# Linear attention by levels of four parts, with TensorE's order around it fixed by dependences

## The chip, the cores and the metric

One Trainium2 chip, one core of it. The program is launched once and computes both layers of the trunk. The metric is the device time of that launch in microseconds (us), lower is better. The core has TensorE (PE, with its weight loads as PEld), VectorE (DVE), ScalarE (ACT), GpSimd (POOL) and the sync engine SP, which issues most DMAs. Each works through its own instructions strictly in program order, and waits on semaphores for the others.

## The reference, cut to what matters

Each of two layers is a SwiGLU half-step, a token mixing and another SwiGLU half-step, on 512 tokens of 1024 channels. Only the mixing is touched:

```python
h = rmsnorm(x, mix_norm[l])
q_a, k_a, v_a, q_b, k_b, v_b, r_b, g_lr, gate_a, gate_b = split_cols(h @ w_in[l], IN_SPLITS)
o_a = swa_attention(...)       # 8 heads of 64, softmax with sinks over a window of 128 tokens
log_a = log_sigmoid(g_lr @ gla_w_gate[l] + gla_gate_bias[l]) / 16
o_b = gla_attention(q_b, k_b, v_b, log_a)   # 4 heads, keys of 128, values of 256
o_b = rmsnorm(o_b) * silu(r_b)
merged = sigmoid(gate_a) * (o_a @ w_proj_a[l]) + sigmoid(gate_b) * (o_b @ w_proj_b[l])
x = x + merged @ w_out[l]

# inside gla_attention, with b the running sum of log_a: for t >= s
attn[t, s] = sum_c q[t, c] * k[s, c] * exp(b[t, c] - b[s, c])
o = attn @ v + (q * exp(b)) @ S     # S: the state that is carried over chunks
```

The decay exp(b[t] - b[s]) differs by channel c, so attn is no single matrix product. The kernel splits it by levels: for a pair t, s on two sides of a boundary r, exp(b[t] - b[r]) goes to q and exp(b[r] - b[s]) to k, and the product of the two is one matmul for all pairs that a boundary of this level parts.

## The kernel before

All tensors lie transposed, channels on the 128 partitions and the 512 tokens along the free axis, in four blocks of 128 tokens. Weights are float32, split into a high and a low part in a narrower format, so that each dense product is three matmuls (`mul3`, L182; operands float32r). The split is one ScalarE copy (`whi`, L114) and one VectorE subtraction (`wlo`, L115) for each 512 columns, in class `Weights`, which also issues the DMA of 1 MB on SP (L133). The small matmuls of the attention and of the linear attention are float32; the hardware runs such a matmul in two passes, which appear as two records, so that "x8" in a row is four matmuls.

A tile scheduler orders the instructions of each engine ahead of time: the earlier something is written, the higher its rank; what stands later in the code is taken where the earlier has not got its operands. `with tc.high_priority` lifts weight loads ahead. PSUM has eight buffers, four of tag `mm` (the dense products, `acc()`) and four of tag `sm` (all the small ones, `psum()`); a matmul into an `sm` buffer waits until the engine that reads its former contents is through.

The mixing, `mix` (L420), is written in this order:

- q and k of the softmax attention, their rotation by `cos` and `sin` (columns of the constants `cst`), `values(0)`.
- The attention, L571 to L613: eight steps (four blocks, two groups of four heads). A step is a chain: eight score matmuls (L581, operands float32r, so one record each), four VectorE reductions with mask and maximum (L586), two tiny ones (L589, L590), five ScalarE exponentials (L591, L594), VectorE sum, reciprocal and four scalings (L595 to L599), TensorE transposes (L606), two VectorE copies (L608), the product with v (L612) and its split (L613).
- The decays b of the linear attention (L616 to L631), q and k of its four heads (`pair`, L635: 48 dense matmuls each), `values(1)` and `values(2)` (L508: 96 dense matmuls of 384 columns each).
- The linear attention, head by head, L647 to L737: seven levels of two parts (widths 64 to 1). A level is VectorE subtractions (L655, L659), an exponential (L198), GpSimd's product with k (L662, into one of three buffers `ke`), VectorE's with q (L666), four matmuls of 64 columns (L675; L671 for width 64) and a masked copy into `attn` (L678). After the levels the diagonal (L683), states (L691 to L712), output (L721, L723), its copy by VectorE (L725), squares, norm and a scaling by VectorE (L736).
- `gate` and the products of the softmax attention's output with its projection, four times (L748 to L759), then everything else (L762 on).

Since gates and projections stand later, the scheduler puts them between the steps of the linear attention, as it puts the q and k products and the values between the steps of the softmax attention.

Of the kernel before, what the change touches and what calls it, by code (L numbers as in the profile page):

```python
# [10 lines left out]
F32R = mybir.dt.float32r  # L11
# [6 lines left out]
P = 128  # L18
# [12 lines left out]
LEVELS = (64, 32, 16, 8, 4, 2, 1)  # L31
# [6 lines left out]
C_ID, C_TRI, C_ONE, C_BO, C_AM, C_COS, C_SIN = 0, 128, 256, 257, 289, 545, 1057  # L38
NCONST = 1569
# [17 lines left out]
def trunk(ctx, tc, xT, wgu, wd, wqk, wv, wg, wpa, wpb, wo, glaw, vecs, consts, masks, out):  # L57
# [49 lines left out]
    cos = cst[:, C_COS:C_COS + T]  # L107
    sin = cst[:, C_SIN:C_SIN + T]
# [73 lines left out]
    def mul3(ps, w, a, start, stop, onto=False):  # L182

        PE.matmul(ps, w[0], a[0], start=start, stop=False, skip_group_check=onto)  # L184
        PE.matmul(ps, w[0], a[1], start=False, stop=False, skip_group_check=onto)  # L185
        PE.matmul(ps, w[1], a[0], start=False, stop=stop, skip_group_check=onto)  # L186


    tables = [None, None]

    def after(ins, before):
        if before is not None:
            tc.add_manual_dep(ins.ins, before.ins.name, mybir.DependencyInfo(
                mybir.DependencyClass.NoSync, mybir.DependencyReason.DATA), reason="in this order")
        return ins

# [223 lines left out]
    def mix(l, norm, nxt, gl):  # L420
# [20 lines left out]

        tables[1] = after(S.preload_act_table_set("natural_log_exp_and_others"), tables[0])
# [12 lines left out]
        def head_tile(i, ps):  # L455
# [11 lines left out]
            if i < 4:  # L467
                z = slot(("qr0", "qr1", "b0", "b1")[i], (P, 2, T), F32R)
# [99 lines left out]

        op = pairs(O, 4, F32R)
# [45 lines left out]

        bp = pairs("b", 2)  # L616
        bT = [bp[h // 2][:, h % 2, :] for h in range(GH)]
        for tb in range(NB):
            t = slice(tb * P, (tb + 1) * P)
            ps = psum()  # L620
            PE.matmul(ps, glr[:, t], gw, start=True, stop=True)
            e, lg = temp(1), temp(2)
            S.activation(e, ps, AF.Abs)
            explog(e, e, AF.Exp, scale=-1.0)
            explog(e, e, AF.Ln, bias=1.0)
            V.scalar_tensor_tensor(lg, ps, 0.0, e, op0=ALU.min, op1=ALU.subtract)
            pb = psum()
            for h in range(GH):
                PE.matmul(pb[:, h * P:(h + 1) * P], lg[:, h * P:(h + 1) * P], tri, start=True, stop=True)
            for z in range(2):  # L630
                S.copy(bp[z][:, :, t], pb[:, z * 256:(z + 1) * 256].rearrange("p (h t) -> p h t", h=2))  # L631


        qb, kb = [], []
        for h in range(GH):  # L635
            for to, tag, ps in zip((qb, kb), "qk", pair(wqk[l, 3 + h])):
                z = slot(f"{tag}{h}")
                S.copy(z, ps)
                to.append(z)
# [5 lines left out]
        onat = []  # L645
        nke = 0
        for h in range(GH):  # L647
            q, k, b, at = qb[h], kb[h], bT[h], attn[h % 2]
            for li, w in enumerate(LEVELS):
                qv, kv, bv = (z.rearrange("p (n s w) -> p n s w", s=2, w=w) for z in (q, k, b))  # L650
                ref = bv[:, :, 0, w - 1:w].broadcast_to([P, T // (2 * w), w])
                dec = temp(1, (P, 2, 256))
                dq, dk = (dec[:, n, :].rearrange("p (n w) -> p n w", w=w) for n in range(2))
                qe = temp(2, (P, 256))
                V.tensor_sub(dq, bv[:, :, 1, :], ref)  # L655
                if w > 1:
                    ke = kes[nke % 3]
                    nke += 1
                    V.tensor_sub(dk, ref, bv[:, :, 0, :])  # L659
                    explog(dec, dec, AF.Exp)  # L660
                    kev = ke.rearrange("p i t -> p (i t)").rearrange("p (n s w) -> p n s w", s=2, w=w)
                    G.tensor_mul(kev[:, :, 0, :], dk, kv[:, :, 0, :])  # L662
                else:
                    ke = k.rearrange("p (i t) -> p i t", i=NB)
                    explog(dq, dq, AF.Exp)
                V.tensor_mul(qe.rearrange("p (n w) -> p n w", w=w), dq, qv[:, :, 1, :])  # L666
                ps = psum()[:, :256].rearrange("p (i t) -> p i t", i=NB)
                if w == 64:

                    for i in range(NB):  # L670
                        PE.matmul(ps[0:w, i, :], ke[:, i, 0:w], qe[:, i * w:(i + 1) * w], start=True, stop=True)  # L671
                    V.tensor_copy(at[0:w, :, w:P], ps[0:w])
                    continue
                for i in range(NB):
                    PE.matmul(ps[:, i, :], ke[:, i, :], qe[:, i * 64:(i + 1) * 64], start=True, stop=True)  # L675
                m = msk[:, li * 64:(li + 1) * 64].rearrange("p (n w) -> p n w", w=w)
                m = m.unsqueeze(1).broadcast_to([P, NB, 64 // w, w])
                V.copy_predicated(at.rearrange("p i (n s w) -> p i n s w", s=2, w=w)[:, :, :, 1, :], m,  # L678
                                  ps.rearrange("p i (n w) -> p i n w", w=w))
# [292 lines left out]
```

## Time and profile before

| | |
|---|---|
| Time, median of 3 runs | 2339.38 us (2338.86 to 2339.99) |
| Time of the profiled execution | 2339.81 us |
| Span of the profiled execution, first to last instruction | 2338.0 us |
| Mean granted TensorE clock | 0.997 |
| PE busy | 2316.0 us (99%) in 13430 records |
| DVE busy | 1592.8 us (68%) |
| ACT busy | 1156.7 us (49%) |
| POOL busy | 159.3 us (7%) |
| HBM read | 215.58 MB, 95 GB/s over the span |

A row of the timeline gives the start, the duration, the engine, the line of the code, the operation and what it writes and reads. Matmuls overlap: a record lasts longer than the distance to the next one, and the distance is what a matmul costs TensorE. The idle time ahead of a group, and what ended it, stands in brackets.

### The profile page before, as it was taken

What the parts mean: (1) busy time and instruction counts of PE and PEld (TensorE: products, weight loads), DVE (VectorE), ACT (ScalarE), POOL (GpSimd) and SP (SyncE); (2) the same over time, 40 slices, a digit from 0 to 9 for tenths busy, and PEclk for the clock granted to TensorE, in tenths of its full rate; (3) what the DMA queues carried; (4) which work ended last, traced back from release to release, by engine and by line L of the source; (5) the groups of instructions that cost most, each with busy time, mean ns of one, the idle gap of its engine ahead of it and who ended that gap; (6) DMA issues with size and microseconds to landing.
All of it is one profiled execution on the core that took longest, in us unless ns stands there. A gap on an engine that the chain in (4) does not pass through costs nothing.

```text
span 2338.0 us, 35293 instructions
## 1 busy us (share of the span) xinstructions
PE 2316.0 (99%) x13430; PEld 2030.5 (87%) x13430; DVE 1592.8 (68%) x2935; ACT 1156.7 (49%) x2167; POOL 159.3 (7%) x150
## 2 busy tenths in 40 slices
PE   9999999999999999999999999999999999999999
PEld 7989988787888889899889899887878888898997
DVE  8948945658665578488478488456596556784882
ACT  5635645454555356256446256454545644552651
POOL 2000010003110100000100000100131101000000
PEclk9999999999999999999999999999999999999999
DMA  5232243211133322323322323431212233222332
GB/s 182 85 112 99 91 143 119 72 68 37 55 98 113 131 73 98 111 91 110 105 84 94 114 91 110 142 110 59 68 37 72 91 125 110 86 97 98 109 103 87
DMA packets 73738, 226.78 MB, mean 97 GB/s; under 512 B 8736, under 2 KB 17056, under 8 KB 73568
## 3 DMA queue, kind: packets, MB, share of 16 engines
q1 hardware_dynamic: 71280, 221.46, 28.1%
q10 hardware_dynamic: 2288, 3.06, 0.5%
q8 instruction: 105, 1.72, 0.3%
q14 instruction: 65, 0.53, 0.1%
HBM read 215.58 MB, written 6.29 MB: 95 GB/s over the span
## 4 chain that ended last, share of the span: by engine, by line
PE 88%; DVE 7%; ACT 2%; DMA 2%; issue 1%; POOL 0%; SPq 0%; DVEq 0%; POOLq 0%; ACTq 0%
PE mm L184 25%; PE mm L185 25%; PE mm L186 25%; PE sm L675 2%; DVE wlo L115 1%; PE sm L184 1%; PE sm L185 1%; PE sm L186 1%; PE mm L519 1%; DMA raw<-in_wgu 1%; PE mm L521 1%; PE mm L520 1%; PE sm L581 1%; PE sm L612 1%; PE sm L606 1%
## 5 line engine op out<-in xcount | busy, mean ns | idle before, releaser
L114 ACT CAST whi<-raw 128x512 fp32r<-128x512 f32 (+1 forms) x1021 | 618.1, 609 | 899.8 <-PE mm L185 746.7
L115 DVE TENSOR_TENSOR wlo<-raw,whi 128x512 fp32r<-128x512 f32 (+1 forms) x1021 | 704.4, 693 | 440.0 <-ACT whi L114 429.9
L184 PE MATMUL mm<-uh,whi 128*128 128x512 f32 (+1 forms) x1448 | 512.3, 355 | 0.9 <-DVE t L388 0.6
L185 PE MATMUL mm<-ul,whi 128*128 128x512 f32 (+1 forms) x1448 | 511.6, 353 | 0.1
L186 PE MATMUL mm<-uh,wlo 128*128 128x512 f32 (+1 forms) x1448 | 508.6, 352 | 0.7 <-DVE wlo L115 0.7
L184 PEld LDWEIGHTS mm<-uh,whi 128*128 128x128 f32 x1448 | 274.4, 190 | 38.9 <-DVE t L381 1.6
L185 PEld LDWEIGHTS mm<-ul,whi 128*128 128x128 f32 x1448 | 275.0, 190 | 36.7 <-DVE ul L221 1.5
L186 PEld LDWEIGHTS mm<-uh,wlo 128*128 128x128 f32 x1448 | 274.4, 189 | 35.9 <-DVE wlo L115 1.5
L185 PE MATMUL mm<-v,whi 128*128 128x512 f32 x640 | 249.1, 389 | 0.0
L185 PEld LDWEIGHTS mm<-v,whi 128*128 128x128 f32 x640 | 120.2, 188 | 24.4
L184 PE MATMUL mm<-k,whi 128*128 128x512 f32 x320 | 124.6, 389 | 0.0
L184 PE MATMUL mm<-q,whi 128*128 128x512 f32 x320 | 124.5, 389 | 0.0
L186 PE MATMUL mm<-k,wlo 128*128 128x512 f32 x320 | 124.5, 389 | 0.0
L186 PE MATMUL mm<-q,wlo 128*128 128x512 f32 x320 | 124.5, 389 | 0.0
L266 POOL TENSOR_TENSOR sum<-sum,t 128x512 f32<-128x512 f32 x42 | 58.7, 1397 | 679.1 <-ACT t L265 385.2
L184 PE MATMUL mm<-b,whi 128*128 128x256 f32 (+1 forms) x332 | 102.9, 310 | 0.1
L186 PE MATMUL mm<-qr,wlo 128*128 128x256 f32 (+1 forms) x332 | 100.7, 303 | 0.0
L186 PE MATMUL mm<-b,wlo 128*128 128x256 f32 (+1 forms) x332 | 100.7, 303 | 0.0
L184 PE MATMUL mm<-qr,whi 128*128 128x256 f32 (+1 forms) x332 | 100.7, 303 | 0.0
L184 PE MATMUL sm<-uh,whi 128*128 128x256 f32 (+1 forms) x284 | 82.2, 289 | 0.0
L185 PE MATMUL sm<-ul,whi 128*128 128x256 f32 (+1 forms) x284 | 82.0, 289 | 0.0
L186 PE MATMUL sm<-uh,wlo 128*128 128x256 f32 (+1 forms) x284 | 82.0, 289 | 0.0
(328 smaller groups left out, 4655.0 us busy)
## 6 DMA issues: line engine op xcount, KB each, us to landing
raw<-in_wgu SPq DMA_DIRECT2D x174, 512.0 KB, 4.3
raw<-in_wd SPq DMA_DIRECT2D x64, 512.0 KB, 3.5
raw<-in_wg SPq DMA_DIRECT2D x48, 512.0 KB, 4.8
raw<-in_wqk SPq DMA_DIRECT2D x26, 512.0 KB, 4.4
raw<-in_wd SPq DMA_DIRECT2D x64, 192.0 KB, 3.7
raw<-in_wpb SPq DMA_DIRECT2D x16, 512.0 KB, 4.7
raw<-in_wo SPq DMA_DIRECT2D x16, 512.0 KB, 5.6
raw<-in_wv SPq DMA_DIRECT2D x16, 384.0 KB, 3.6
```

The source lines that it names most:

```text
L114: S.copy(hi, src)
L115: V.tensor_sub(lo, src, hi.bitcast(F32))
L184: PE.matmul(ps, w[0], a[0], start=start, stop=False, skip_group_check=onto)
L185: PE.matmul(ps, w[0], a[1], start=False, stop=False, skip_group_check=onto)
L186: PE.matmul(ps, w[1], a[0], start=False, stop=stop, skip_group_check=onto)
L266: G.tensor_tensor(self.sum, self.sum, sq, op=ALU.add)
L519: PE.matmul(ps, u[k][0][:, t], wh, start=k == 0, stop=False)
L520: PE.matmul(ps, u[k][0][:, t], wl, start=False, stop=False)
L521: PE.matmul(ps, u[k][1][:, t], wh, start=False, stop=k == KD - 1)
L581: PE.matmul(ps[half][:, j, k0:], stacked[2 * jp + j][:, half, t], z[:, half, n * P - P + k0:(n + 1) * P], start=z is kh, stop=z is kl)
L606: row = after(PE.transpose(pt[:, kc, j, :], s[half][:, j, kc * P:(kc + 1) * P], ident), row)
L675: PE.matmul(ps[:, i, :], ke[:, i, :], qe[:, i * 64:(i + 1) * 64], start=True, stop=True)
```

## The change

The linear attention is divided into functions: `prepare(h)` (all of VectorE's, ScalarE's and GpSimd's work ahead of the matmuls), `upper(h)`, `lower(h)` (the matmuls of the levels, the states) and `output(h)`.

The levels have four parts instead of two: widths 32, 8 and 2 (three boundaries each) and 1, in place of 64, 32, 16, 8, 4, 2 and 1. Width 32 is 12 small matmuls a head (32 columns of weights; 96, 64 and 32 columns moving, at three positions in the array); widths 8 and 2 are four matmuls each, of 192 columns; each half of such a level is copied by three masked copies.

The decays b and the q and k products of the four heads are written ahead of the softmax attention. After it come `values(1)`, `values(2)` and then the linear attention and the gates in one explicit order: every matmul that is written after a `fence()` depends on the last one written before it, without a semaphore, so that the scheduler can't move it ahead. Head 0's matmuls are not fenced. The table of `cos` and `sin` moves out of the constants into a buffer `cs` that is loaded once a layer by SP and is then reused for the exponentials of q; the projection comes in four loads of 0.5 MB instead of two of 1 MB. The copy of the output and its scaling move from VectorE to ScalarE.

```diff
+    fenced, newest = [None], [None]
+    def mat(*args, **kw):
+        newest[0] = after(PE.matmul(*args, **kw), fenced[0])
+        return newest[0]
+    def fence(on=True):
+        fenced[0] = newest[0] if on else None
     def mul3(ps, w, a, start, stop, onto=False):
-        PE.matmul(ps, w[0], a[0], start=start, stop=False, skip_group_check=onto)
+        mat(ps, w[0], a[0], start=start, stop=False, skip_group_check=onto)
...
+        with tc.high_priority(offset=PREP):
+            turn = slot("cs", (P, 2, T))
+            nc.sync.dma_start(turn.rearrange("p i t -> p (i t)"), consts[:, NCONST:])
...
+        def prepare(h):
+            q, k, b = qb[h], kb[h], bT[h]
+            for li, w in enumerate(QUARTERS):
...
+                dk = temp(1, (P, 3 * P))
+                V.tensor_sub(dk.rearrange("p (n s w) -> p n s w", s=3, w=w),
+                             ends[:, :, 0:3, w - 1:w].broadcast_to([P, P // w, 3, w]), ends[:, :, 0:3, :])
+                explog(dk, dk, AF.Exp)
...
+                e = slot(("cs", "gb" if h else f"{X}3", f"{X}3" if h else "cs")[li], (P, 2, T))
...
+                for a in range(3):
...
+                    V.tensor_sub(z, bv[:, :, :, (a + 1) * w:], bv[:, :, :, (a + 1) * w - 1:(a + 1) * w].broadcast_to(
+                        [P, NB, 32 // w, (3 - a) * w]))
+                explog(e, e, AF.Exp)
+                for a, z in enumerate(parts):
...
+                    V.tensor_mul(z, z, qv[:, :, :, (a + 1) * w:])
...
+        def level(h, li):
...
+            for half in range(2):
...
+                ps = psum()[:, :384].rearrange("p (i c) -> p i c", i=2)
+                for i in range(2):
+                    mat(ps[:, i, :], ke[:, 2 * half + i, :], e[:, (2 * half + i) * 192:(2 * half + i + 1) * 192],
+                        start=True, stop=True)
+                for a in range(3):
...
+                    V.copy_predicated(
...
-                V.tensor_copy(o, ps)
+                S.copy(o, ps)
...
-                V.tensor_scalar(z, z, to[:, n, :], None, op0=ALU.mult)
+                S.activation(z, z, AF.Copy, scale=to[:, n, :])
...
+        prepare(0)
+        upper(0)
+        lower(0)
+        output(0)
+        for h in range(1, GH):
+            prepare(h)
+            fence()
+            open_gate(h - 1)
+            fence()
+            if h > 1:
+                output(h - 1)
+            upper(h)
+            fence()
+            through(h - 1)
+            fence()
+            lower(h)
+        fence()
+        open_gate(3)
+        fence()
+        output(3)
+        through(3)
+        fence(False)
```

Lines of the changed code in what follows: scores L624, reductions L629, transposes L649, product with v L655, `mat` and `turned` L191 and L195. `open_gate(b)` is 48 dense matmuls, `through(b)` 24.

TensorE's order before, around the transposes (L606) of the seventh of eight attention steps in the first layer; `mm_5069` to `mm_5072` are sums of `values(1)`:

```order
L519 MATMUL mm_5071<-whi_5146,uh5_3684 128x384
L520 MATMUL mm_5071<-wlo_5147,uh5_3684 128x384
L521 MATMUL mm_5071<-whi_5146,ul5_3685 128x384
L519 MATMUL mm_5072<-whi_5146,uh5_3684 128x384
L606 MATMUL sm_4644<-cst_80,t1_4626 128x128 x4
L606 MATMUL sm_4651<-cst_80,t1_4625 128x128 x4
L520 MATMUL mm_5072<-wlo_5147,uh5_3684 128x384
L521 MATMUL mm_5072<-whi_5146,ul5_3685 128x384
```

Between the scores and the transposes of each of the eight steps stand 20 to 38 dense matmuls in this order. TensorE's order after, at the sixth step; there `sm_4917` and `sm_4918` hold its scores, `sm_4946` and `sm_4953` its transposes, `sm_4960` its product with v, and `sm_4971` is of the seventh:

```order
L624 MATMUL sm_4917<-gb_4299,x1_4093 128x256
L624 MATMUL sm_4918<-ga_4298,x1_4093 128x256
L624 MATMUL sm_4918<-gb_4299,x1_4093 128x256
L649 MATMUL sm_4946<-cst_80,t1_4928 128x128 x4
L649 MATMUL sm_4953<-cst_80,t1_4927 128x128 x4
L655 MATMUL sm_4960<-t2_4958,va1_4117 64x256
L655 MATMUL sm_4960<-t2_4951,va1_4117 64x256
L655 MATMUL sm_4960<-t2_4958,va2_4118 64x256
L655 MATMUL sm_4960<-t2_4951,va2_4118 64x256
L624 MATMUL sm_4971<-ga_4298,qr0_3976 128x256
```

The dense matmuls are gone from here. In the first five steps 28, 31, 34, 35 and 37 of them stand between scores and transposes, and 5, 5, 7, 10 and none between transposes and product; in the sixth, seventh and eighth none stands anywhere. The second layer has the same order.

TensorE's order before, in the linear attention's second head (L671 and L675 are its levels of width 64, 32 and 16; `mm_6050` and `mm_6064` are the projection's sums):

```order
L186 MATMUL mm_6050<-o1_4308,wlo_5969 128x512
L184 MATMUL mm_6064<-o0_4307,whi_5955 128x512
L671 MATMUL sm_5510<-t2_5504,ke0_3812 64x64 x4
L675 MATMUL sm_5523<-t2_5517,ke1_3813 128x64 x4
L675 MATMUL sm_5536<-t2_5530,ke2_3814 128x64 x4
L185 MATMUL mm_6064<-o2_4309,whi_5955 128x512
L186 MATMUL mm_6064<-o0_4307,wlo_5956 128x512
```

TensorE's order after, in head 0, which follows the eighth attention step:

```order
L191 MATMUL sm_5418<-x3_5371,ke1_3813 128x192 x2
L191 MATMUL sm_5424<-x3_5371,ke1_3813 128x192 x2
L195 MATMUL sm_5430<-cst_80,ksd_5396 128x128 x3
L191 MATMUL sm_5436<-cs_5383,ke2_3814 128x192 x2
L191 MATMUL sm_5442<-cs_5383,ke2_3814 128x192 x2
L191 MATMUL sm_5448<-t2_5392,k0_4442 128x64 x4
L191 MATMUL sm_5454<-q0_4440,k0_4442 128x128 x4
L191 MATMUL sm_5464<-v0_4112,kt_5434 128x256
```

From the scores of the sixth attention step to the end of head 0's output TensorE's queue holds no dense matmul; the first dense one after it is `open_gate(0)`'s. In heads 1 to 3 dense ones stand only as the two blocks of 48 and 24 that the fences leave.

VectorE's order after, in head 1, while TensorE runs `through(0)`: the masked copies of head 1's level of width 8 (L753) stand behind the sum inside the gate's sigmoid (L217), which needs three ScalarE passes of 1024 columns after `open_gate(0)`:

```order
L675 TENSOR_TENSOR t1_6027<-b1_4310 128x384
L217 SCALAR_TENSOR_TENSOR x0_5552<-qr0_5551,x0_5552 128x1024
L753 COPY_PREDICATED attn1_3811<-msk_81,sm_5645 128x8x24
L753 COPY_PREDICATED attn1_3811<-msk_81,sm_5651 128x8x24
L753 COPY_PREDICATED attn1_3811<-msk_81,sm_5645 128x8x16
```

Before, the same sum (there L205) stood between masked copies of the second and third head as well. The number of masked copies a head goes from six (and one plain copy) to 14.

## Rows read from the trace of the kernel before

**Rows 1.** The page's busy times: engine, us (share of the span), instructions

```profile
PE 2316.0 (99%) x13430; PEld 2030.5 (87%) x13430; DVE 1592.8 (68%) x2935; ACT 1156.7 (49%) x2167; POOL 159.3 (7%) x150
```

**Rows 2.** Waits of PE: line, waited for, us in total, times, longest

```profile
PE sm L671 <- DVE t L666: 4.7, 2, 2.4
```

**Rows 3.** Windows over the linear attention, both layers: length, busy us, clock, DMA

```profile
520.00:620.00 100.00, 94.00 (x529) 78.57 (x528) 84.57 (x182) 45.45 (x99) 32.95 (x36) 0.97 0.12 43
1684.00:1784.00 100.00, 93.98 (x529) 78.58 (x528) 84.57 (x182) 45.55 (x99) 32.56 (x35) 0.97 0.13 43
```

**Rows 4.** Timeline, first layer, one attention step: start, us, engine, line, operation

```profile
463.45 1.08 PE L612 MATMUL sm<-t,va 128*64 128x256 f32 x8
...
464.46 0.38 PE L581 MATMUL sm<-ga,b 128*128 128x256 f32 x1
...
465.48 0.54 DVE L586 CUSTOM_DVE_ANT_0 t<-sm,cst,vec 128x256 f32<-128x256 f32 x1
...
467.35 0.08 DVE L586 DVE_READ_ACCUMULATOR2_ANT mx<- 128x1 f32 x1
...
467.82 0.16 DVE L589 TENSOR_SCALAR nmx<-mx 128x4 f32<-128x4 f32 x1
...
468.49 0.21 ACT L198 ACTIVATE es<-es 128x4 f32<-128x4 f32 x1
...
470.70 0.16 DVE L595 TENSOR_TENSOR es<-es,rs 128x4 f32<-128x4 f32 x1 [2.66 <-ACT t L198]
...
471.11 0.35 DVE L599 TENSOR_SCALAR t<-t,es 128x256 f32<-128x256 f32 x1
...
471.85 0.87 DVE L599 TENSOR_SCALAR t<-t,es 128x256 f32<-128x256 f32 x3
...
472.87 1.06 PE L606 MATMUL sm<-cst,t 128*128 128x128 f32 x8
...
473.53 0.69 DVE L608 COPY t<-sm 128x512 f32<-128x512 f32 x1
...
475.45 1.08 PE L612 MATMUL sm<-t,va 128*64 128x256 f32 x8
```

**Rows 5.** Timeline of PE in the same step: two dense matmuls of the values

```profile
468.66 0.34 PE L520 MATMUL mm<-wlo,uh 128*128 128x384 f32 x1
468.84 0.34 PE L521 MATMUL mm<-whi,ul 128*128 128x384 f32 x1
```

**Rows 6.** Timeline of PE at the start of the linear attention, first layer

```profile
523.43 0.65 PE L671 MATMUL sm<-t,ke 128*64 128x64 f32 x8 [2.34 <-DVE t L666]
524.01 3.22 PE L675 MATMUL sm<-t,ke 128*128 128x64 f32 x16
...
527.99 0.63 PE L184 MATMUL mm<-uh,whi 128*128 128x512 f32 x1
528.42 0.63 PE L185 MATMUL mm<-ul,whi 128*128 128x512 f32 x1
```

**Rows 7.** Timeline of PE later in the same head

```profile
538.22 1.06 PE L675 MATMUL sm<-t,k 128*128 128x64 f32 x8
539.11 1.11 PE L683 MATMUL sm<-q,k 128*128 128x128 f32 x8
...
542.52 1.03 PE L721 MATMUL sm<-v,attn 128*128 128x256 f32 x4
543.38 0.59 PE L723 MATMUL sm<-ga 128*128 128x256 f32 x2
```

**Rows 8.** Single lines: engine, operation, count, ns least/median/most, first and last start

```profile
L655 DVE TENSOR_TENSOR t<-b x56: 398/417/955, 518.6 to 1768.2; 128x256 f32<-128x256 f32 x56
L692 DVE TENSOR_TENSOR ksd<-b x8: 545/546/557, 513.3 to 1753.0; 128x384 f32<-128x384 f32 x8
L202 ACT ACTIVATE x<-qr x8: 1042/1062/1064, 547.9 to 1896.3; 128x1024 f32<-128x1024 f32 x8
L662 POOL TENSOR_TENSOR ke<-t,k x48: 722/756/1082, 520.9 to 1767.9; 128x256 f32<-128x256 f32 x48
```

More of the change, by code (lines that the diff above doesn't have):

```diff
@@ L613, in mix @@
                 split(oah[jp][:, :, t], oal[jp][:, :, t], av.rearrange("p (h t) -> p h t", h=2))
[L616 to L631, printed above, removed]
@@ L634, in mix @@
[L634 to L639, printed above, removed]
         values(1)
         values(2)
[L645 to L679, printed above, removed]
-            ps = psum().rearrange("p (i t) -> p i t", i=NB)
-            for i in range(NB):
-                t = slice(i * P, (i + 1) * P)
-                PE.matmul(ps[:, i, :], k[:, t], q[:, t], start=True, stop=True)
-            V.copy_predicated(at, msk[:, 448:576].unsqueeze(1).broadcast_to([P, NB, P]), ps)
@@ L696, in mix, with upper @@
             explog(eb, b3[:, 0:3, P - 1], AF.Exp)
-            vc = slice(h * 256, (h + 1) * 256)
+            states[h] = ksd, eb
+        def upper(h):
+            at, w = attn[h % 2], QUARTERS[0]
+            ke, e, parts = levels[h, w]
+            ps = psum()
+            for i in range(NB):
+                for a, z in enumerate(parts):
+                    n = (3 - a) * w
+                    mat(ps[a * w:(a + 1) * w, i * n:(i + 1) * n], ke[:, i, a * w:(a + 1) * w], z[:, i, :],
+                        start=True, stop=True)
+            for a in range(3):
+                n = (3 - a) * w
+                own = slice(a * w, (a + 1) * w)
+                S.copy(at[own, :, (a + 1) * w:], ps[own, :4 * n].rearrange("p (i c) -> p i c", i=NB))
+            level(h, 1)
+            ksd, eb = states[h]
@@ new lines, in lower @@
+        def lower(h):
+            q, k, b, at = qb[h], kb[h], bT[h], attn[h % 2]
+            level(h, 2)
+            qe = levels[h, 1]
+            ps = psum()[:, :256].rearrange("p (i t) -> p i t", i=NB)
+            for i in range(NB):
+                mat(ps[:, i, :], k[:, i * P:(i + 1) * P], qe[:, i * 64:(i + 1) * 64], start=True, stop=True)
+            V.copy_predicated(at.rearrange("p i (n s) -> p i n s", s=2)[:, :, :, 1],
+                              msk[:, 384:448].unsqueeze(1).broadcast_to([P, NB, 64]), ps)
+            ps = psum().rearrange("p (i t) -> p i t", i=NB)
+            for i in range(NB):
+                t = slice(i * P, (i + 1) * P)
+                mat(ps[:, i, :], k[:, t], q[:, t], start=True, stop=True)
+            V.copy_predicated(at, msk[:, 448:576].unsqueeze(1).broadcast_to([P, NB, P]), ps)
+            qs = slot("sum", (P, 3 * P))
+            explog(qs, b[:, P:], AF.Exp)
+            G.tensor_mul(qs, qs, q[:, P:])
+            vc = slice(h * 256, (h + 1) * 256)
+            kt, eb = states[h]
+            gs = slot("ga" if h else f"{X}2", (P, 2, T)).rearrange("p i t -> p (i t)")
@@ L705, in mix @@
                 ps = psum()[:, :256]
-                PE.matmul(ps, kt[:, n, :], v[n][:, vc], start=True, stop=True)
+                mat(ps, kt[:, n, :], v[n][:, vc], start=True, stop=True)
                 s1 = gs[:, n * 256:(n + 1) * 256]
@@ L712, in mix, with output @@
                 st.append(s1)
+            states[h] = st, qs
+        def output(h):
+            at = attn[h % 2]
+            st, qs = states[h]
+            vc = slice(h * 256, (h + 1) * 256)
             so = slot("so", (P, NB, 1), bufs=2)
```

128 lines of the change are left out of this document (93 added, 35 removed).

## The prediction

> **What bounds the kernel now.** I read the page's busy times first: TensorE is busy 99% of the span, VectorE 68% [rows 1]. A busy TensorE may still be slow, so the next views are its waits and the windows with the granted clock. What there is to win lies in one place, the linear attention of each layer: in 100 us there TensorE is busy 94.0, and the clock is 0.97 [rows 3]. The largest wait is the first, 4.7 us in two times, one a layer: the first level's matmuls wait for VectorE's product with q [rows 2]. Behind it dense matmuls start 0.43 us apart [rows 6], the lower of the clock's two levels (1.2 GHz). A layer thus loses 6.0 us of idleness and 0.03 * 100 = 3 us of clock, together 9 us; 18 us in both.
>
> Everywhere else TensorE sets the pace because something fills its waits. The timeline of one attention step shows it: from its scores to the next product with v pass 11 us, and TensorE's own work in it is about 3 us; dense matmuls fill the rest [rows 4, 5].
>
> **The change, part by part.**
>
> *TensorE's own work.* Removed are five levels of four matmuls of 64 columns, in 4 heads and 2 layers: 160 matmuls, 320 records, at (539.11 - 538.22) / 8 = 0.111 us [rows 7], 35.6 us; and 32 of width 64 (64 records at (524.01 - 523.43) / 8 = 0.073 [rows 6]), 4.6 us. Added are 64 matmuls of 192 columns. The trace has none; its neighbours are 0.111 a record (64 columns) and (543.38 - 542.52) / 4 = 0.215 (256 columns) [rows 7]. In proportion to the latter 192 columns cost 0.161: 128 records, 20.6 us (14 to 27). Added too are 96 matmuls with 32 columns of weights. The nearest row, 64 columns of weights, gives 0.073 a record as an upper bound; the product with v, which works in two halves of the array, needs (464.46 - 463.45) / 8 = 0.126 for 256 columns instead of 0.215 [rows 4, 7], so positions run beside each other. I take 0.04: 192 records, 7.7 us (5 to 14). TensorE saves 40.2 - 28.3 = 12 us (0 to 21).
>
> *The old stalls.* Head 0's q side is prepared before the attention, and the following heads have 48 and 24 dense matmuls as cover. I let all 18 us go (10 to 18); what is late next is below.
>
> *The end of the softmax attention.* This decides. The q and k products, formerly filling, now rank ahead and are used up before the first scores; 192 matmuls of the values are left for eight steps, and TensorE's order has them gone after the fifth. Since its queue is strict, it waits in the sixth to eighth step for the chain. The chain from product to product with v, without others' work in it [rows 4]: 463.45 to the first reduction at 465.48, 2.03 us; four reductions to 467.43, 1.95; one small operation, 0.2; five exponentials on ScalarE from 468.49 to 470.67, 2.2; sum and reciprocal 0.4; four scalings 0.35 + 0.87, less overlap, 1.15; 0.15 to the transposes; 0.66 to the first copy; two copies 1.4; 0.2 to the product. Sum 10.3 us. TensorE's own part is 1.0 + 1.06 + 0.95 = 3.0, so it idles 7.3 us; three times 22. The fifth step adds its gap between transposes and product, 475.45 - 472.87 - 0.95 = 1.6 us. In the eighth VectorE has ten operations of head 0 and 1 between the links (0.4 to 0.55 us each [rows 8]), partly beside the exponentials: 1.6 more. Together 25 us a layer at the full clock. One idleness of 2.34 us was followed by the lower clock [rows 6]; here each is longer, so the tail should run low, which lengthens product and half of the transposes by 1.4 us a step: 29. I take 28 (23 to 31).
>
> *Its first five steps.* From scores to transposes 8.4 us passed (464.46 to 472.87 [rows 4]); at 0.18 us a matmul [rows 5] plus 1.06 of scores, 34, 35 and 37 of them cover 7.2 to 7.7. With the small steps of the first block and the gap behind the transposes 4.5 us (2 to 7). The decays' chains, between 14 to 17 matmuls of the q and k products each, about 1.5 (0 to 3), an estimate from half of L202's 1.06 for three passes of 512 columns and a VectorE pass.
>
> *Head 0.* Its matmuls follow directly, and no dense one is among them. TensorE's part is about 10 us. VectorE's chain: first level's matmuls 1, three subtractions for the level of width 2 1.25 (546 ns for 384 columns, 417 for 256 [rows 8]; the buffer `cs` is free only then), exponential 0.9, three products 1.25, matmuls 0.7, eight masked copies with subtractions of head 1 between them about 5, state 0.5, output 3.0 (14 records at 0.215 [rows 7]): about 15 us. So 5 us idle at the full clock, 8 at the lower: 6 (4 to 9). The lower clock then outlasts the tail into `open_gate(0)`, 2 us (0 to 3.4).
>
> *Heads 1 to 3.* The masked copies of width 8 stand behind the sigmoid's sum, that is behind three ScalarE passes of 1.06 us [rows 8] and what ScalarE has between them (copies and squares of the output). Four `sm` buffers are then held, and TensorE reaches the states 1 to 3 us too early in each of three heads: 5 us a layer (0 to 10). Copy and scaling of the output cost nothing on ScalarE, which is 45% busy there [rows 3], unless they lie in this chain; that is in the 5. The load of `cs` and the split projection are a few 0.5 MB more or less on SP: nothing, with a DMA share of 0.12 in these windows [rows 3].
>
> GpSimd's products fall from 8 to 5 a head. In the trace a VectorE subtraction of 417 ns took up to 955 [rows 8] while GpSimd was at work. The Trainium skill, "SBUF — State Buffer" (its paragraph on the shared port pair), calls that pair an exclusive lock for a whole instruction. By that rule 24 instructions fewer give VectorE 24 times about 0.54 us, 13 us in both layers, and if heads 1 to 3 hung on VectorE alone, their 10 us would be gone and the sum 2393. The order shows them hanging on ScalarE's sigmoid and on `sm` buffers, so I keep them.
>
> **Sum.** New waits a layer: 28 + 4.5 + 1.5 + 6 + 2 + 5 = 47; two layers 94. Against the profiled execution's 2339.81 us (span 2338.0 and 1.8 around it; 0.4 above the median): 2339.8 - 12 - 18 + 94 = 2403.8, on the median's footing 2403.
>
> **The rivals.**
>
> *The full clock* in the tail (the idle stretches alternate with bursts of 1 to 2 us, and the trace has only single ones): 25 + 5 + 0 + 11 = 41 a layer, 2339.4 - 30 + 82 = 2391. For it: the shorter waits in the same 100 us (6.0 less 2.34 us of idleness) left the clock up, since 0.97 is no more than one low stretch [rows 2, 3]. Against it: 7 us is thrice what went ahead of that one. The Trainium skill ("TensorE: Matmul & The Clock Gate", section "A second HAM failure mode: psum-queue depth-cycling") tells of a kernel whose clock swings between the levels as TensorE idles between groups of matmuls; by that half of the tail would run low, which gives 2397; no run here shows it yet.
>
> *VectorE and ScalarE bind in heads 1 to 3:* VectorE is 85% busy in these windows already [rows 3], and the masked copies go from six to 14 a head. If each of three heads loses 5 us more: 2403 + 30 = 2433.
>
> *Faster:* the tail costs nothing, since VectorE and ScalarE, with no splits of weights in the sixth to eighth step, run the chain faster than TensorE can notice. Then the savings win: 2339.4 - 12 - 18 = 2309, and with head 0's stall 2321. It decides where the chain falls from 10.3 to about 5 us a step: gains of 15 us a layer, less 7 for head 0, leave 8 for three steps with 3.0 of own work. Against it: ScalarE's exponentials and VectorE's reductions and scalings alone are 2.2 + 1.95 + 1.15 + 1.4 = 6.7 us, each waiting for the one before.
>
> *The change doesn't do what its words say:* head 0 would then run beside the attention in name only, its matmuls all behind the last step. The order says just this, so it is part of the forecast.
>
> **How the numbers follow.** Forecast (2403, its own terms 2380 to 2420) 0.5; full clock 0.26; VectorE and ScalarE binding 0.16; faster 0.05; savings and stalls about even 0.03. The low end takes the full clock with savings of 21 and the small terms at their low ends: 2339 - 21 - 18 + 2 * 33 = 2366; the high end is the binding rival near 2433. A difference of 0.2% is about what a measurement of this kernel can tell from no change, so "same" is 2335 to 2344: faster 0.05, same 0.03, slower 0.92.
>
> **What would show it.** In the profile after: transposes and products of the sixth to eighth step with idle time of about 7 and 1.5 us ahead of them, released by the scalings (L642) and the copies (L651); a lower clock around them; waits of head 0's matmuls for VectorE; no wait of 2.3 us ahead of the first level. Wrong it would be if TensorE's busy share stays at 99%, or if the waits lie mainly in heads 1 to 3.

## The result, and the profile after

The changed kernel takes 2406.7 us (2406.1 to 2407.6, four runs); the kernel before beside it 2339.1 (2338.2 to 2340.0). The ratio is 1.0289, with a 95% interval from 1.0272 to 1.0307: slower by 67.6 us. Both profiles show where. The page of the changed kernel gives TensorE's busy share first, which was 99% [rows 1]:

```profile
PE 2321.6 (97%) x13366; PEld 2036.2 (85%) x13366; DVE 1588.0 (66%) x2959; ACT 1185.8 (49%) x2239; POOL 147.1 (6%) x126
```

Its largest waits of TensorE (engine, line, what was waited for: us in total, times, longest). The 4.7 us of the first level [rows 2] are no longer among them; transposes (L649) and products with v (L655) of the softmax attention lead instead:

```profile
PE sm L649 <- DVE t L642: 40.4, 10, 7.9
PE sm L191 <- DVE attn L753: 16.6, 6, 3.6
PE sm L655 <- DVE t L651: 6.6, 8, 0.9
```

To place the time I cut the mixing part of the first layer into three stretches by TensorE's instructions: A goes from the transposes of the decays' input to the first scores, B from there to the end of the last product with v, C from there to the first transposes of the heads' outputs. Work may move from one to another, so the sum is what compares. The windows of the kernel before, then of the changed one (window: length, busy us and instructions of PE, PEld, DVE, ACT and POOL, granted clock, DMA share, GB/s):

```profile
406.40:412.00 5.60, 5.60 (x38) 3.82 (x35) 4.42 (x11) 4.35 (x11) 0.00 (x0) 1.00 0.55 187
412.00:498.40 86.40, 86.10 (x476) 69.69 (x475) 53.79 (x178) 40.50 (x120) 0.00 (x0) 1.00 0.18 62
498.40:651.50 153.10, 147.07 (x791) 124.30 (x792) 110.04 (x220) 77.19 (x156) 34.20 (x37) 0.98 0.18 62
```

```profile
408.20:460.70 52.50, 51.07 (x250) 41.08 (x249) 23.45 (x46) 32.21 (x69) 2.26 (x2) 1.00 0.21 76
460.70:550.40 89.70, 64.73 (x372) 54.26 (x373) 56.09 (x183) 35.75 (x114) 3.24 (x3) 0.81 0.14 45
550.40:685.20 134.80, 125.22 (x653) 104.79 (x654) 87.22 (x193) 70.30 (x148) 22.48 (x20) 0.94 0.17 59
515.00:551.00 36.00, 16.36 (x83) 11.25 (x85) 20.73 (x62) 11.48 (x39) 3.24 (x3) 0.51 0.00 1
590.90:597.70 6.80, 5.15 (x12) 4.00 (x13) 6.35 (x20) 0.58 (x2) 0.00 (x0) 0.50 0.23 80
```

The sum went from 245.1 to 277.0, 32 us a layer, and the second layer shows the same (244.8 and 277.0): nearly the whole loss lies here. In B TensorE now idles 25.0 of 89.7 us, before 0.3 of 86.4. The fourth row is the end of B: 36 us at 1.2 GHz (0.51 of full speed), with 16.4 us busy. The timeline of TensorE there (start, us, line, out<-in; in brackets the idle time ahead and who ended it) repeats three times:

```profile
510.50 1.08 PE L655 MATMUL sm<-t,va 128*64 128x256 f32 x8 [0.94 <-DVE t L651]
...
518.62 1.94 PE L649 MATMUL sm<-cst,t 128*128 128x128 f32 x8 [5.89 <-DVE t L642]
521.34 1.97 PE L655 MATMUL sm<-t,va 128*64 128x256 f32 x8 [0.78 <-DVE t L651]
...
531.08 1.94 PE L649 MATMUL sm<-cst,t 128*128 128x128 f32 x8 [5.76 <-DVE t L642]
533.80 1.98 PE L655 MATMUL sm<-t,va 128*64 128x256 f32 x8 [0.78 <-DVE t L651]
...
545.69 1.94 PE L649 MATMUL sm<-cst,t 128*128 128x128 f32 x8 [7.91 <-DVE t L642]
548.42 1.98 PE L655 MATMUL sm<-t,va 128*64 128x256 f32 x8 [0.78 <-DVE t L651]
```

From product to product a step takes 10.8, 12.5 and 14.6 us, with nothing between scores and transposes, where the kernel before had its dense matmuls [rows 4, 5]. In stretch C the largest wait stands in head 1 (first fence). The second fence is VectorE at the same time:

```profile
587.82 1.11 PE L191 MATMUL sm<-q,k 128*128 128x128 f32 x8
592.55 2.90 PE L191 MATMUL sm<-v,kt 128*128 128x256 f32 x6 [3.62 <-DVE attn L753]
```

```profile
584.43 1.21 DVE L217 SCALAR_TENSOR_TENSOR x<-qr,x 128x1024 f32<-128x1024 f32 x1
585.57 1.27 DVE L753 COPY_PREDICATED attn<-msk,sm 128x192 f32<-128x192 uint8 x6
...
587.23 0.68 DVE L843 TENSOR_TENSOR x<-x,mm 128x512 f32<-128x512 f32 x1
587.82 2.83 DVE L114 TENSOR_TENSOR wlo<-raw,whi 128x512 fp32r<-128x512 f32 x2
590.58 0.67 DVE L843 TENSOR_TENSOR x<-x,mm 128x512 f32<-128x512 f32 x1
591.17 1.37 DVE L753 COPY_PREDICATED attn<-msk,sm 128x192 f32<-128x192 uint8 x6
```

The level of width 2 (two buffers), the pairs and the diagonal hold all four `sm` buffers. The states' matmuls (`sm<-v,kt`) need one, and the copies that free it (591.17) stand on VectorE behind the projection's products (L843) and two splits. Then the clock is down for 6.8 us (the last row of the windows, 590.90 to 597.70, at 0.50). Head 2 has the same with a wait of 2.72 us and 3.3 us at 0.50.

### The profile page after: what moved, and what is told of

Same layout as the page of the kernel before. It is cut to its first block, busy times and chain, and to the rows that moved or that the text cites. A ratio compares the mean times of both kernels' runs of the same rounds, so it can differ in the third digit from the quotient of the medians.

```text
span 2405.3 us, 35114 instructions
## 1 busy us (share of the span) xinstructions
PE 2321.6 (97%) x13366; PEld 2036.2 (85%) x13366; DVE 1588.0 (66%) x2959; ACT 1185.8 (49%) x2239; POOL 147.1 (6%) x126
## 5 line engine op out<-in xcount | busy, mean ns | idle before, releaser
L191 PE MATMUL mm<-uh,whi 128*128 128x512 f32 (+1 forms) x1448 | 514.1, 356 | 4.1 <-ACT v L545 2.1
L191 PE MATMUL mm<-uh,wlo 128*128 128x512 f32 (+1 forms) x1448 | 508.4, 351 | 0.7 <-DVE wlo L114 0.7
L191 PE MATMUL mm<-ul,whi 128*128 128x512 f32 (+1 forms) x1448 | 508.8, 352 | 0.0
L191 PEld LDWEIGHTS mm<-uh,whi 128*128 128x128 f32 x1448 | 275.2, 190 | 43.3 <-DVE t L393 2.9
L191 PEld LDWEIGHTS mm<-uh,wlo 128*128 128x128 f32 x1448 | 275.0, 190 | 37.9 <-DVE wlo L114 1.5
L191 PEld LDWEIGHTS mm<-ul,whi 128*128 128x128 f32 x1448 | 275.1, 190 | 37.6 <-DVE ul L233 1.4
L191 PE MATMUL mm<-v,whi 128*128 128x512 f32 x640 | 249.1, 389 | 0.0
L191 PEld LDWEIGHTS mm<-v,whi 128*128 128x128 f32 x640 | 120.2, 188 | 24.5
L191 PE MATMUL mm<-b,whi 128*128 128x256 f32 (+1 forms) x600 | 134.6, 298 | 1.0 <-ACT t L392 0.9
L191 PE MATMUL mm<-qr,whi 128*128 128x256 f32 (+1 forms) x600 | 132.8, 294 | 0.0
L191 PE MATMUL mm<-k,whi 128*128 128x512 f32 x320 | 124.6, 389 | 0.0
L191 PE MATMUL mm<-q,whi 128*128 128x512 f32 x320 | 124.5, 389 | 0.0
L191 PE MATMUL mm<-k,wlo 128*128 128x512 f32 x320 | 124.5, 389 | 0.0
L191 PE MATMUL mm<-q,wlo 128*128 128x512 f32 x320 | 124.5, 389 | 0.0
L191 PE MATMUL mm<-o,whi 128*128 128x512 f32 x320 | 104.3, 391 | 0.0
L191 PE MATMUL mm<-x,whi 128*128 128x512 f32 x320 | 104.2, 391 | 0.0
L191 PEld LDWEIGHTS mm<-b,whi 128*128 128x128 f32 x600 | 95.3, 191 | 8.5 <-ACT t L392 4.0
L191 PE MATMUL mm<-qr,wlo 128*128 128x256 f32 (+1 forms) x332 | 100.7, 303 | 0.0
L191 PE MATMUL mm<-b,wlo 128*128 128x256 f32 (+1 forms) x332 | 100.7, 303 | 0.0
```

The source lines that it names most:

```text
L191: newest[0] = after(PE.matmul(*args, **kw), fenced[0])
```

## The experiments

All were timed beside the kernel before (2338.1 us, 2337.7 in the last four). A, B and C are the stretches of the first layer in us; they come from the windows of the profiled execution. That of h_order_behind was the slowest of its nine (2334.7), and its second layer takes 236.5.

| kernel | median us | ratio, 95% interval | A | B | C | sum |
|---|---|---|---|---|---|---|
| before | 2339.1 | | 5.6 | 86.4 | 153.1 | 245.1 |
| changed | 2406.7 | 1.0289 (1.0272, 1.0307) | 52.5 | 89.7 | 134.8 | 277.0 |
| a_qk_behind | 2364.6 | 1.0108 (1.0093, 1.0124) | 29.9 | 91.1 | 135.4 | 256.4 |
| b_levels_alone | 2354.2 | 1.0064 (1.0049, 1.0079) | 5.6 | 86.3 | 158.6 | 250.5 |
| c_no_fence | 2340.0 | 1.0007 (0.9998, 1.0017) | 52.7 | 87.8 | 104.2 | 244.7 |
| d_states_mm | 2381.6 | 1.0188 (1.0173, 1.0203) | 52.7 | 89.7 | 123.6 | 266.0 |
| e_filled | 2386.7 | 1.0208 (1.0193, 1.0224) | 52.8 | 83.9 | 130.8 | 267.5 |
| f_free | 2321.6 | 0.9928 (0.9913, 0.9943) | 29.9 | 89.2 | 115.0 | 234.1 |
| g_gate0 | 2353.8 | 1.0066 (1.0049, 1.0083) | 30.0 | 89.2 | 132.4 | 251.6 |
| h_order_behind | 2331.1 | 0.9971 (0.9961, 0.9981) | 5.6 | 86.3 | 150.2 | 242.1 |
| i_output_vector | 2403.8 | 1.0284 (1.0267, 1.0301) | 52.7 | 89.8 | 134.7 | 277.2 |
| j_two_repairs | 2341.0 | 1.0015 (1.0006, 1.0024) | 30.1 | 91.1 | 123.6 | 244.8 |
| k_free_mm | 2335.8 | 0.9991 (0.9982, 1.0000) | 29.9 | 91.2 | 120.9 | 242.0 |
| l_free_vector | 2330.1 | 0.9966 (0.9955, 0.9978) | 30.2 | 89.1 | 121.8 | 241.1 |

**Is the loss the bare end of the attention?** Behind the attention, ahead of `values(1)`, stand again:

```diff
-        for h in range(GH):
-            for to, tag, ps in zip((qb, kb), "qk", pair(wqk[l, 3 + h])):
+        products(0)
...
+        for h in range(1, GH):
+            products(h)
         values(1)
```

> One part undone: the q and k products of heads 1 to 3 (144 dense matmuls a layer, 32.7 us at 0.227) stand behind the softmax attention again; head 0's products and the decays stay ahead. In TensorE's order each of the first seven steps of the attention now has 24 to 49 dense matmuls, the eighth 13, where the changed kernel has none in the sixth to eighth. Theory (the bare end of the attention is the loss): of its 22.8 us of waits a layer about 4 stay in the eighth step, and with the clock up its own work and head 0's are some 6 us shorter: 25 a layer, 2357 us (2345 to 2372). Rival (heads 1 to 3, their fences and sm buffers): no more than 10 us in all, 2397 or above. Rival (the levels of four parts cost VectorE what TensorE saves, wherever the products stand): above 2397 too.

Measured: 2364.6, 42 us less than the changed kernel. Its waits for the transposes (line L652 there) fall from 40.4 to 15.6 us, those in C stay:

```profile
PE sm L191 <- DVE attn L758: 17.7, 6, 3.6
PE sm L652 <- DVE t L645: 15.6, 6, 6.1
PE sm L658 <- DVE t L654: 3.1, 2, 1.5
```

The eighth step keeps 6.1 us, 2 more than I expected. C is as long as before this repair (135.4 and 134.8). So the end of the attention is 42 us of the 68, and a second loss lies in C.

**What does the clock cost there?** In the sixth to eighth step:

```diff
-                    pt = psum().rearrange("p (k h t) -> p k h t", k=2, h=2)
+                    pt = psum()
+                    if half and 2 * n + jp > 4:
+                        row = last
+                        for i in range(26):
+                            row = after(PE.matmul(pt, u[i % KD][0][:, :P], u[i % KD][0], start=True, stop=True), row)
+                    pt = pt.rearrange("p (k h t) -> p k h t", k=2, h=2)
```

> The changed kernel with 26 matmuls of 512 columns more (5.9 us at 0.227) between scores and transposes in each of the sixth to eighth step of the attention; their results are overwritten and used by nothing. They fill TensorE's wait without shortening the chain on VectorE and ScalarE, so what the time does is the price of the lower clock. Theory (the low clock lengthens steps of 10.3 us to 12.5 and 14.6 and keeps head 0 slow): 4 to 8 us a layer less, 2395 (2389 to 2400). Rival (only latency: the chain sets the steps at either clock): 2404 to 2409. Rival (the added matmuls delay the transposes): above 2410.

Measured: 2386.7, 20 us less, although TensorE does 18 us more a layer. Its timeline, the added matmuls in line L650:

```profile
507.63 1.08 PE L660 MATMUL sm<-t,va 128*64 128x256 f32 x8 [0.94 <-DVE t L656]
...
509.70 6.08 PE L650 MATMUL sm<-uh 128*128 128x512 f32 x26
515.67 1.09 PE L654 MATMUL sm<-cst,t 128*128 128x128 f32 x8
517.71 1.08 PE L660 MATMUL sm<-t,va 128*64 128x256 f32 x8 [0.94 <-DVE t L656]
...
527.84 1.08 PE L660 MATMUL sm<-t,va 128*64 128x256 f32 x8 [0.94 <-DVE t L656]
...
540.86 1.97 PE L660 MATMUL sm<-t,va 128*64 128x256 f32 x8 [0.78 <-DVE t L656]
```

The steps are now 10.1, 10.1 and 13.0 us: the same chain, 4.7 us shorter over three steps, and B is 5.8, C 4.0 us shorter. That is the clock's price, some 10 us a layer, and a little less than all of it: in the third of these steps the wait of 2.1 us and the lower clock are back (its product lasts 1.97 us again). If only latency counted, nothing would have been gained. My 4 to 8 a layer was too low, since I had left out most of what follows the attention.

**What do the fences cost?** `fence()` never sets anything:

```diff
-        fenced[0] = newest[0] if on else None
+        fenced[0] = None
```

> The changed kernel without its fences; everything is written where it was, but the scheduler may draw the gates' matmuls forward. Its order then has 29, 8 and 30 dense matmuls in the sixth, seventh and eighth step of the attention. Theory (bare end): about two thirds of 22.8 us of waits a layer go, with some 5 us of clock: 2363 (2355 to 2380), with the seventh step's wait of about 5 us left. Rival (what the fences order in heads 1 to 3 is worth more than the filled tail): 2400 or above.

Measured: 2340.0, 67 us less, all of the loss, while the products stand where the change put them. Its windows B and C:

```profile
460.30:548.10 87.80, 80.32 (x457) 67.33 (x455) 59.52 (x186) 42.38 (x122) 3.20 (x3) 0.94 0.17 58
548.10:652.30 104.20, 98.92 (x569) 82.64 (x568) 79.31 (x191) 63.33 (x138) 25.19 (x20) 1.00 0.19 66
```

In B the idle time falls from 25.0 to 7.5 us, since gates' matmuls fill the sixth and eighth step, and in C from 9.6 to 5.3. Of the 32 us a layer these are 22; the other 10 are the clock (0.81 to 0.94 in B, 0.94 to 1.00 in C). The waits:

```profile
PE sm L649 <- DVE t L642: 10.3, 6, 4.5
PE sm L195 <- POOL ksd L711: 5.6, 4, 1.5
PE sm L191 <- ACT attn L730: 3.5, 4, 1.5
```

For the masked copies (L753) TensorE now waits 0.6 us in all. My estimate had counted the tail alone and was 23 us too high for that reason.

**What is the loss in C?** Only the states' buffers:

```diff
-                ps = psum()[:, :256]
+                ps = acc()[:, :256]
                 mat(ps, kt[:, n, :], v[n][:, vc], start=True, stop=True)
```

> The changed kernel with the states' matmuls in the mm buffers instead of the sm buffers, which the masked copies hold. Theory (in heads 1 and 2 TensorE waits 3.6 and 2.7 us for an sm buffer and then runs 6.8 and 3.4 us at the lower clock): the waits for a masked copy (16.6 us in six times) fall to below 6, and the time by 10 to 20: 2392. Rival (VectorE's queue is what everyone waits for, and the next matmul waits as long): 2404 to 2408.

Measured: 2381.6, 25 us less, more than the 10 to 20 expected. VectorE's queue is as it was, so the four `sm` buffers were what TensorE waited for; the end of the attention is untouched (B again 89.7):

```profile
PE sm L649 <- DVE t L642: 40.5, 10, 7.9
PE sm L655 <- DVE t L651: 6.6, 8, 0.9
PE sm L191 <- DVE attn L773: 3.5, 2, 1.8
```

C falls from 134.8 to 123.6, its clock rises from 0.94 to 0.99. Waits of 8.3 us a layer went (1.9 in head 0, 3.6 and 2.7 in heads 1 and 2) and about 3.4 came (1.2 for `kt`, 1.1 more for L773, 1.1 for L843); the rest of the 11 us (6 us of shorter busy time) is clock.

**Do the two losses add?** Edits a and d together, fences kept.

> Two repairs with the fences kept: q and k products of heads 1 to 3 behind the attention (a_qk_behind) and the states' matmuls in the mm buffers (d_states_mm). Theory (two losses in different places, which add): 2407 less 42 and 25 is 2340 (2333 to 2346), with only the eighth step of the attention still waiting; the fences then cost nothing else but that step's cover. Rival (with the fences' order the next buffer or VectorE's queue takes over): 2350 or above.

Measured: 2341.0, against 2339.5 by adding. So the two are separate, and together nearly all of the loss. The 67 us of c_no_fence are no third loss: without fences other matmuls fill the same two places.

**Both, without the fences.** Edits a and c together.

> Both repairs together: q and k products of heads 1 to 3 behind the attention (a_qk_behind), and no fences (c_no_fence). In TensorE's order all eight steps of the attention then have dense matmuls, the eighth 13 of the values and 26 of a gate. Theory (the end of the attention and the fenced heads are two separate losses): from the 2340 of c_no_fence its 11.9 us of waits for L642 and L651, and most of its 17 us at the lower clock (6 us), go too: 2325 (2316 to 2333), below the kernel before. Rival (without fences the scheduler only shifts the same matmuls; what it puts into the attention is missing as cover in the heads): 2336 to 2345.

Measured: 2321.6, 0.9928 of the kernel before (0.9913 to 0.9943) and the fastest here. Its page, its largest waits and its windows B and C:

```profile
PE 2293.0 (99%) x13366; PEld 2014.1 (87%) x13366; DVE 1576.2 (68%) x2959; ACT 1183.5 (51%) x2239; POOL 153.7 (7%) x126
```

```profile
PE sm L652 <- DVE t L645: 3.5, 4, 1.6
PE sm L658 <- DVE t L654: 3.1, 2, 1.5
PE sm L195 <- POOL ksd L716: 2.3, 2, 1.2
```

```profile
437.00:526.20 89.20, 85.79 (x500) 72.44 (x501) 62.52 (x197) 44.61 (x129) 4.69 (x4) 1.00 0.20 63
526.20:641.20 115.00, 112.36 (x627) 93.80 (x628) 84.48 (x200) 69.74 (x148) 25.78 (x20) 1.00 0.21 69
```

No wait is longer than 1.6 us and the clock is full throughout.

**The fences alone, once the end is filled.** a_qk_behind, with

```diff
+        open_gate(0)
         prepare(0)
...
             fence()
-            open_gate(h - 1)
-            fence()
+            if h > 1:
+                open_gate(h - 1)
+                fence()
```

> a_qk_behind with the first gate's products written ahead of head 0 and unfenced, so that the eighth step of the attention is filled as in f_free; the fences between the heads from head 1 on stay as in the changed kernel. Theory: the wait of 6.1 us in the eighth step and the low clock behind it go, 8 us a layer against a_qk_behind, and some of it comes back where this gate's 48 products stood as cover in head 1 (3 us): 2355 (2348 to 2362). The difference to f_free is then the price of the fences in heads 1 to 3, some 30 us in both layers. Rival (the fences cost nothing by themselves): within 5 us of f_free.

Measured: 2353.8. B equals that of f_free (89.2), C is 17.4 us longer. Its two largest waits:

```profile
PE sm L191 <- DVE attn L758: 12.9, 4, 4.5
PE sm L191 <- DVE cs L702: 11.1, 2, 5.6
```

The first, for the masked copies (0.9 us in f_free), is the fenced heads'. The second (1.6 us in f_free) stands in head 0, which has no fence: its q products now stand on VectorE behind the gate, and the clock is low for 6.8 us around this wait. So the edit brought a loss of its own, and the 17.4 us are an upper bound of the fences' price, not the price itself.

**What do the levels alone bring?** Decays and all q and k products stand behind the attention again. In b_levels_alone the heads and gates follow as in the diff; h_order_behind keeps the sequence of the change there, with each head prepared ahead, but without fences:

```diff
-        prepare(0)
...
-        fence(False)
+        for h in range(GH):
+            prepare(h)
+            upper(h)
+            lower(h)
+            output(h)
+        for b in range(4):
+            open_gate(b)
+            through(b)
```

> The levels of four parts alone, in the order of the kernel before: decays and all q and k products behind the attention, each head's steps one after the other, the gates behind all heads, nothing fenced. Theory: only TensorE's own saving is left, 12 us of 2339 (0 to 21), and a first level that still waits: 2327 (2316 to 2340). Rival (the levels themselves are the loss, since 14 masked copies a head keep VectorE): 2360 to 2400.

> Decays and all q and k products behind the attention, as in the kernel before, but each head prepared ahead of the outputs and states of the last one and the gates written between the heads, nothing fenced. Against b_levels_alone it adds the preparing ahead; against f_free it lacks head 0's preparing beside the attention. Theory (b_levels_alone lost its 12 us and 16 more because a head's decay tiles are written only when the last head is done): the waits for the q products of 4.6 and 2.0 us in heads 1 to 3 go, 10 us a layer, and head 0's first wait with its clock stays: 2335 (2328 to 2343). Rival (VectorE's longer work in the levels sets the pace): 2350 to 2358.

Measured: 2354.2 and 2331.1. Alone the levels lose 16 us. The waits of b_levels_alone, then of h_order_behind:

```profile
PE sm L191 <- DVE gb L696: 13.0, 4, 4.6
PE sm L195 <- POOL ksd L710: 7.4, 5, 3.0
PE sm L191 <- DVE cs L696: 6.2, 7, 1.8
```

```profile
PE sm L195 <- POOL ksd L710: 6.8, 4, 4.1
PE sm L191 <- DVE cs L696: 4.6, 4, 1.9
```

The tiles of a head's levels (`gb`, `cs`) exist once, and in b_levels_alone TensorE waits for them up to 4.6 us. In h_order_behind the waits for `gb` are gone. It differs from b_levels_alone in two things, the preparing ahead and the gates written between the heads; the two together are worth 23 us, and only with them do the levels gain: 7 us. What each gives was not separated. The 9.5 us from there to f_free are what preparing head 0 beside the attention, with decays and products ahead of it, adds.

**Smaller parts.** Copy and scaling of the output on VectorE again, in the changed kernel and in f_free; and f_free with the states in the `mm` buffers:

```diff
-                S.copy(o, ps)
+                V.tensor_copy(o, ps)
...
-                S.activation(z, z, AF.Copy, scale=to[:, n, :])
+                V.tensor_scalar(z, z, to[:, n, :], None, op0=ALU.mult)
```

> The changed kernel with one part undone: copy and scaling of the output (two copies of 512 columns and four scalings of 256 a head) on VectorE again. Theory (they lie beside other work on either engine, as the prediction said): 2403 to 2411. Rival (on ScalarE they delay the sigmoid, behind which VectorE's masked copies of heads 1 and 2 stand): 2395 to 2402. Rival (VectorE binds in heads 1 to 3): above 2412.

> f_free with copy and scaling of the output on VectorE again. Theory (with TensorE 99% busy neither engine is waited for long): 2318 to 2327. Rival (VectorE is the busier of the two in the heads, so moving them off it is part of what makes f_free fast): 2328 or above.

> f_free with the states' matmuls in the mm buffers as well. Theory (without fences the scheduler has dense matmuls between, so that the sm buffers no longer hold TensorE up: its waits for masked copies are 0.9 us in all): the same, 2318 to 2325. Rival (buffers still cost something that shows in no wait): below 2317. Rival (states in the mm buffers take them from the gates' products): 2326 or above.

Measured: 2403.8, within the interval of the changed kernel, so there the move is worth nothing. In f_free it is worth 8.5 us (2330.1), so the rival of l_free_vector came true: where nothing else holds TensorE up, VectorE's share is on the path (TensorE waits 3.8 us for the copy itself, and 4.0 instead of 2.3 us for `ksd`). The second rival of k_free_mm came true: 2335.8, 14 us lost. In its order the eighth step has 13 dense matmuls, in that of f_free 39; in its B TensorE is idle 9.5 us instead of 3.4 (clock 0.96). The likely reason, argued from the order and not tested, is that the gate's products that filled the step take `mm` buffers too, and those are now given to the states first. The edit that gained 25 us in one order costs 14 in another. Against j_two_repairs, the same kernel with fences (2341.0), k_free_mm is only 5 us faster: with the states in the `mm` buffers the fences cost little, so most of their price elsewhere is paid at the `sm` buffers and in the eighth step.

## Why the prediction was right, and where a term was off

The forecast was 2403, the time 2406.7; the segment lost 32 us a layer, as summed (47 - 9 - 6). The mechanism is the one forecast: the bare end of the attention first, then the `sm` buffers in the fenced heads. That the sum came out so close is partly luck, since its terms missed by more, in both directions.

- *Own work, 12 us in both layers.* The matmuls of 192 columns start 0.163 us apart at the median (0.161 assumed), those with 32 columns of weights 0.033 (24 in 0.78 us; 0.04 assumed). 128 * 0.163 + 192 * 0.033 = 27.2, so 13.0 us are saved. (That a float32 matmul takes two passes is more than the trace tells: it leaves two records, but each of them costs 0.215 us for 256 columns, where the one record of a float32r matmul costs 0.12.)
- *Old stalls, 18 us.* They went.
- *The end of the attention, 28 a layer.* Three steps of 37.9 us together, less 9.0 of own work, and 0.94 in the fifth: 29.9. The waits of 5.9 and 5.8 plus 0.78 answer to the 7.3 of the chain; its 10.3 us is 10.1 in e_filled. The clock's part within the three steps was put at 4 and measured as at least 4.7.
- *The first five steps, 4.5.* Too high: TensorE waits 1.3 us, once, for the evacuation of values by ScalarE, and 0.4 for the scalings of the fifth step, 1.7 in all. The dense matmuls covered the chains.
- *The decays' chains, 1.5.* The amount came (1.4) in another place: for the decays' chains TensorE waits 0.2 us, for ScalarE's evacuation of the first values 1.2.
- *Head 0, 6.* From 550.3 to the first dense matmul at 566.5 pass 16.2 us, with the 10 of own work 6.2. The size fits by luck: only 2.6 us of it are idle, where 5 were forecast (the links listed for VectorE's chain add to 13.6 us, not 15, which leaves 3.6), and some 3.2 are the clock, low until 553.3 and again, behind a wait of 1.94 us, from 556.7 to 560.2.
- *The low clock into* `open_gate(0)`*, 2.* It did not happen; the clock is at 1.00 from 560.2 on, and the matmuls there start 0.23 us apart from the second on.
- *Heads 1 to 3, 5 (0 to 10).* The term that was too small. Waits of 3.6 and 2.7 us are 6.3, and behind each the clock is low, for 6.8 and 3.3 us with 5.2 and 3.3 of them busy: 4.2 more, 10.5 in all. The forecast had the waits (5) but no clock behind them. It also named the copies of width 8 behind the sigmoid; the ones that hold TensorE up are those of width 2, behind the projection.

So two overestimates (2.8 and 2.0) nearly cancelled what the last term lacked (5.5). By these numbers the terms give 49.7 a layer, less 15.5 is 34.2 against 31.9 measured; 2.3 us a layer stay unassigned. (The low end of the range has a slip of its own: by the terms' low ends its 33 us a layer are 32. Nothing hangs on it.)

Of the rivals, the full clock in the tail fell with the window at 0.51, and e_filled shows roughly what it would have given: 2387, where 2391 was worked out. The Trainium skill ("TensorE: Matmul & The Clock Gate", section "A second HAM failure mode: psum-queue depth-cycling") tells of a clock that swings between its levels; in this trace it did not swing in the tail, but stayed low from 515.8 to 553.3 through three bursts of work. With half of the tail low, as I had worked out from that rule, the time would have been 2397. In d_states_mm, where this tail has the same order and the same waits, the clock did come back, to 1.00 for 3.4 us from 523.1. TensorE was idle there (0.03 us busy from 523.2 to 526.4), so no matmul ran faster by it, and B is 89.7 us in both. Whether the clock swings is thus not fixed by the order; what was priced is the clock under the matmuls.

VectorE and ScalarE as the bound in heads 1 to 3 fell with d_states_mm, where a buffer gives back 25 us without taking work from either. (That rival's count is not like with like: with the diagonal's, the masked copies a head go from seven to 14.) "Beside the attention in name only" holds for TensorE in every version, f_free included, whose first matmul of head 0 stands at 526.13, behind the last product at 525.12; what runs beside is VectorE's preparing.

Whether VectorE got the 13 us that fewer products on GpSimd might have given can't be read from its busy time (1588.0 us after 1592.8), since other work changed too: the copy and scaling that moved to ScalarE are 21.0 us alone (1609.0 in i_output_vector). What is left of the collision shows in one place. In the wait of head 1 the two splits of 512 columns take 2.83 us, while the median of that line is 0.691 each; GpSimd is at work beside them:

```profile
587.75 1.00 POOL L711 TENSOR_TENSOR ksd<-ksd,k 128x384 f32<-128x384 f32 x1 [6.13 <-ACT ksd L210]
588.70 1.40 POOL L679 TENSOR_TENSOR ke<-t,k 128x384 f32<-128x384 f32 x1
```

Each split ends about 0.55 us after a product of GpSimd that it overlaps (588.75 and 589.29, 590.10 and 590.65). So the trace agrees with the Trainium skill ("SBUF — State Buffer", section "SBUF: two separate sides", which calls the port pair shared by VectorE and GpSimd an exclusive lock for a whole instruction). The splits take 1.4 us more than twice the median, ahead of the copies that TensorE waits for; how much shorter its 3.62 us would be without that, no run shows.

What was not separated: fences and the order of the gates' matmuls in C were only taken away together, so the price of the fences by themselves stays open.

## What to carry to other kernels

Dense matmuls that nobody waits for are a store of cover: before moving them ahead, count how many each later chain still finds, in TensorE's final order. An order fixed by dependences must leave that cover free to move; the same levels and the same preparation were 2.9% slower fenced and 0.7% faster with the products behind and no fences. And where a wait is named after an engine, try the buffer first: one line in the states' buffers gave 25 us, though the same line cost 14 us in the order of f_free.

## What the runs showed of the hardware that I had not expected

In the changed kernel waits of 3.6 and 2.7 us inside otherwise busy stretches cost about two thirds of themselves again in clock (6.3 us of waits, 4.2 us lost at the low level). The ratio is no rule: in g_gate0 a wait of 4.5 us was followed by 3.4 us at the low level, in h_order_behind one of 1.9 us by 6.8. In f_free waits of up to 1.6 us left the clock at 1.00. And 18 us of useless matmuls a layer made the kernel 20 us faster, because the work around them ran at the higher level.
